# A row softmax that is bound by its transfers: tiles of twelve rows in four buffers instead of eight rows in six, with a held first store and an uninterleaved end

## The chip, the cores and the metric

The program runs on one core of one Trainium2 chip. The time is device microseconds of one execution. "Span" is the time from the first to the last instruction in a profile; the reported time is some two microseconds longer.

## The reference

```python
batch, seq, dim = 32, 512, 1024          # x: float32, temperature 0.5
scaled  = x / temperature
shifted = scaled - np.max(scaled, axis=-1, keepdims=True)
exp_x   = np.exp(shifted)
return exp_x / np.sum(exp_x, axis=-1, keepdims=True)
```

That is 16,384 rows of 1,024 float32: 67.11 MB are read and 67.11 MB are written.

## The kernel before

A tile holds eight consecutive rows in each of 128 partitions, so one partition's part of a transfer is one piece of 8 x 4 KB = 32 KB. Six such tiles are in flight. A tile is worked on in groups of four rows: VectorE takes the maximum of the group, ScalarE computes the exponentials in place and their sums, VectorE divides. Loads are issued from SyncE (the load queue), stores from ScalarE (the store queue). The load that refills a buffer waits for the store that empties it.

```python
TILES = [[8]] * 16
BUFS = 6
GROUP = 4
...
def load():                                    # next tile, if there is one
    xt = data.tile([P, sum(TILES[i]), d], f32, name="xt")
    nc.sync.dma_start(out=xt, in_=dram(xf, i))
...
def store(g):                                  # after the last group of a tile
    ...
    nc.scalar.dma_start(out=dram(of, i)[:, a : a + k, :], in_=tiles[i][:, a : a + k, :])
    if a + k == sum(TILES[i]):
        load()
...
for _ in range(BUFS):
    load()
for g in range(len(groups) + 1):
    if g < len(groups):
        maximum(g); exponential(g)             # group g ...
    if g > 0:
        divide(g - 1); store(g - 1)            # ... before the division of group g-1
```

## Time and profile before

| | kernel before |
|---|---|
| time, median of 6 runs (lowest to highest) | 317.98 us (317.84 to 318.26) |
| span of the profiled run | 316.0 us |
| loads plus stores, share of the transfer engines' time | 49.7% + 49.2% |
| VectorE, ScalarE busy | 75%, 47% |

The prediction below shows the page's first parts and the rates by window. The rows of the busy instructions, from the page's part 5 of the kernel before, are these (line, engine, operation, output and input with their shapes, count; busy us and mean ns of one; idle time before them and what ended it):

```profile
L79 ACT ACTIVATE xt<-xt,bias 128x1024 f32<-128x1024 f32 x128 | 145.4, 1137 | 136.8 <-DVE recip L91 119.4
L70 DVE TENSOR_REDUCE top<-xt 128x4 f32<-128x4096 f32 x32 | 141.3, 4416 | 62.6 <-DMA xt<-in_x_dram 62.6
L93 DVE TENSOR_SCALAR xt<-xt,recip 128x1024 f32<-128x1024 f32 x128 | 87.7, 749 | 1.1
```

A group of four rows costs VectorE 4.42 us for the maximum, 2.74 us for four divides (overlapping a little) and two small operations: one group starts 7.4 us after the last. VectorE's long waits are all for loads. So VectorE waits for the transfers; the prediction shows that the transfers hardly ever pause.

### The profile page before, as it was taken

How to read it: one execution, taken by the hardware profiler on the slowest of the kernel's cores; microseconds unless marked ns; L12 is line 12 of the kernel's file. 1: busy time of each engine (PE TensorE's matmuls, PEld its weight loads, DVE VectorE, ACT ScalarE, POOL GpSimd, SP SyncE). 2: the span in 40 equal slices, each digit the busy share in tenths (PEclk: the TensorE clock that was granted, in tenths of full speed). 3: DMA queues.
4: the chain of work that ended last, by engine and by line, in shares of the span. 5: the costliest groups of instructions: out<-in, count | busy, mean ns of one | idle time of the engine just before them, and what ended most of it. 6: DMA issues, size and time to landing. Idle time of an engine off the chain costs nothing.

```text
span 316.0 us, 620 instructions
## 1 busy us (share of the span) xinstructions
DVE 235.5 (75%) x224; ACT 149.6 (47%) x257; POOL 0.2 (0%) x4
## 2 busy tenths in 40 slices
DVE  0399999999689494994949859497693976949720
ACT  0176666666526255361554605546064560645500
POOL 0000000000000000000000000000000000000000
DMA  8999999999999999999999999999999999999996
GB/s 332 411 452 423 373 460 415 452 425 431 436 427 440 427 444 423 444 419 448 415 452 411 452 408 456 423 444 427 436 431 432 440 423 444 419 444 419 452 411 274
DMA packets 4612, 134.25 MB, mean 425 GB/s; under 512 B 512, under 2 KB 512, under 8 KB 512
## 3 DMA queue, kind: packets, MB, share of 16 engines
q1 hardware_dynamic: 2304, 67.11, 49.7%
q10 hardware_dynamic: 2304, 67.11, 49.2%
q14 instruction: 4, 0.03, 0.0%
HBM read 67.11 MB, written 67.11 MB: 425 GB/s over the span
## 4 chain that ended last, share of the span: by engine, by line
DVE 49%; DMA 32%; another core or an unknown queue 9%; ACT 5%; issue 1%; DVEq 0%; SPq 0%
DVE top L70 29%; DMA xt<-in_x_dram 20%; DVE xt L93 18%; DMA out_dram<-xt 12%; ACT xt L79 5%; DVE recip L91 1%; DVE bias L73 1%; DVEq L147 0%; SPq L61 0%
## 5 line engine op out<-in xcount | busy, mean ns | idle before, releaser
L79 ACT ACTIVATE xt<-xt,bias 128x1024 f32<-128x1024 f32 x128 | 145.4, 1137 | 136.8 <-DVE recip L91 119.4
L70 DVE TENSOR_REDUCE top<-xt 128x4 f32<-128x4096 f32 x32 | 141.3, 4416 | 62.6 <-DMA xt<-in_x_dram 62.6
L93 DVE TENSOR_SCALAR xt<-xt,recip 128x1024 f32<-128x1024 f32 x128 | 87.7, 749 | 1.1
L79 ACT ACTIVATION_READ_ACCUMULATOR xt<-xt,bias 128x1 f32 x128 | 23.9, 187 | 0.0
L79 ACT ACT_TABLE_LOAD x1 | 1.3, 1283 | 13.0 <-DMA xt<-in_x_dram 13.0
L91 DVE RECIPROCAL recip<-sums 128x4 f32<-128x4 f32 x32 | 5.5, 171 | 2.1 <-ACT xt L79 2.1
L73 DVE TENSOR_SCALAR bias<-top 128x4 f32<-128x4 f32 x32 | 5.4, 170 | 1.1
L133 POOL MEMSET const-bfloat16-1.0<- 128x1 bf16 x1 | 0.1, 101 | 0.0
L133 POOL MEMSET const-uint8-127<- 128x1 uint8 x1 | 0.1, 101 | 0.0
L133 POOL MEMSET const-float32-0.0<- 128x1 f32 x1 | 0.1, 98 | 0.2 <-issue 0.2
L133 POOL MEMSET const-float32-1.0<- 128x1 f32 x1 | 0.1, 98 | 0.0
## 6 DMA issues: line engine op xcount, KB each, us to landing
xt<-in_x_dram SPq DMA_DIRECT2D x16, 4096.0 KB, 50.2
out_dram<-xt ACTq DMA_DIRECT2D x16, 4096.0 KB, 38.6
```

Of the source, the lines that this page charges most:

```text
L70: nc.vector.tensor_reduce(out=top, in_=tiles[i][:, a : a + k, :], axis=mybir.AxisListType.X, op=extreme)
L73: nc.vector.tensor_scalar_mul(bias, in0=top, scalar1=-scale)
L79: nc.scalar.activation(tiles[i][:, a + b, :], tiles[i][:, a + b, :], mybir.ActivationFunctionType.Exp, bias=bias[:, b : b + 1], scale=scal ...
L91: nc.vector.reciprocal(recip, sums)
L93: nc.vector.tensor_scalar_mul(tiles[i][:, a + b, :], in0=tiles[i][:, a + b, :], scalar1=recip[:, b : b + 1])
L133: nc = _bacc.Bacc("TRN2", target_bir_lowering=False, num_devices=1)
```

## The change

The intent, as far as the diff tells it: fewer, longer transfers with the same 48 rows (192 KB per partition) in the buffers; a first store that doesn't start before the third load is in; and an end in which the store of the tenth tile needn't wait for the eleventh's maximum.

```diff
-TILES = [[8]] * 16
-BUFS = 6
+TILES = [[12]] * 10 + [[8]]
+BUFS = 4
@@ store
             a, k = part
+            if i == 0:
+                nc.scalar.copy(stats.tile([P, 1], f32, name="seen"), tiles[2][:, 0, 0:1])
             nc.scalar.dma_start(out=dram(of, i)[:, a : a + k, :], in_=tiles[i][:, a : a + k, :])
@@ main loop
+            alone = 0 < g < len(groups) and groups[g][0] > groups[g - 1][0] == len(TILES) - 2
+            if alone:
+                divide(g - 1)
+                store(g - 1)
             if g < len(groups):
                 maximum(g)
                 exponential(g)
-            if g > 0:
+            if g > 0 and not alone:
                 divide(g - 1)
                 store(g - 1)
```

The added copy reads one column of the third tile. It stands in ScalarE's order ahead of the store, so ScalarE reaches the store only when that tile has landed.

## The prediction

> **What bounds the kernel now.** I read the page of the profile first, for the share of each engine; then the rates in chosen windows of time, for where the transfers lose; then the waits of the load-issuing queue and the timelines of the start and the end.
>
> The page, parts 1 to 3 (engine, busy us, share; then tenths and GB/s in 40 slices; then the transfer queues):
>
> ```profile
> span 316.0 us, 620 instructions
> DVE 235.5 (75%) x224; ACT 149.6 (47%) x257; POOL 0.2 (0%) x4
> DMA  8999999999999999999999999999999999999996
> GB/s 332 411 452 423 373 460 415 452 425 431 436 427 440 427 444 423 444 419 448 415 452 411 452 408 456 423 444 427 436 431 432 440 423 444 419 444 419 452 411 274
> q1 hardware_dynamic: 2304, 67.11, 49.7%
> q10 hardware_dynamic: 2304, 67.11, 49.2%
> ```
>
> Two queues, loads (q1) and stores (q10), together take 98.9% of the sixteen transfer engines' time. No compute engine passes 75%. The kernel is bound by moving 67.11 MB in and 67.11 MB out, not by VectorE, although the chain that ended last names it for 49%: that chain runs through whatever came last at each step, while the transfers beside it never pause.
>
> The windows view (stretch, its length, busy time of each engine, clock, transfer share, GB/s) says where bytes were not moved:
>
> ```profile
> 0.00:2.50 2.50, 0.00 (x0) 0.00 (x0) 0.20 (x4) 1.00 0.76 210
> 2.50:12.00 9.50, 0.00 (x0) 0.00 (x0) 0.00 (x0) 1.00 0.90 386
> 31.60:39.50 7.90, 7.83 (x9) 5.15 (x11) 0.00 (x0) 1.00 0.97 373
> 120.00:280.00 160.00, 120.17 (x116) 78.42 (x136) 0.00 (x0) 1.00 1.00 433
> 302.00:313.00 11.00, 0.34 (x1) 0.00 (x0) 0.00 (x0) 1.00 0.99 429
> 313.00:316.00 3.00, 0.00 (x0) 0.00 (x0) 0.00 (x0) 1.00 0.05 22
> ```
>
> Over 160 us of the middle the rate is 433 GB/s with the share at 1.00: this is the full rate. Against it each stretch loses its length times (1 - rate/433): the start 1.3 + 1.0 = 2.3 us, the stretch in which the first store joins the loads 1.1 us, the end after 313 us 2.85 us, the rest sums to about -0.4 us (rounding of where packets are counted). Check: 134.22 MB / 433 GB/s = 310.0 us, and 316.0 - 310.0 = 6.0 us against 5.9 us summed. So **six microseconds in all are not full-rate transfer**, and only part of them can be had.
>
> The last store and the issue of loads:
>
> ```profile
> 302.38 0.34 ACTq L101 DMA_DIRECT2D out_dram<-xt  x1
> SPq L61 <- DMA out_dram<-xt: 224.5, 10, 53.8
> ```
>
> Each of the ten later loads waits for a store to free its buffer, 224.5 us in total. That costs nothing today: a 4 MB load takes 50.2 us (median) from issue to landing, though it moves in 9.7 us at full rate, so it stands in a long line. The last store goes out at 302.38 us, while the store before it is still moving (429 GB/s in 302 to 313 us), so the end is just covered too.
>
> **What the Trainium skill says.** "DMA: Bandwidth & Descriptors", section "Where 436 GB/s comes from", gives 435.2 GB/s as the ceiling of the ports; this case's 433 agrees, so the middle has no more to give. "HBM Reference", section "Specifications (TRN2)", says that a core alone measures about 425 GB/s, bounded by its 16 DMA engines; the page's mean is 425. "DMA: Bandwidth & Descriptors", section "Queues, rings and completion order", says each DMA engine alternates between its queues packet by packet; the trace agrees: the first load lands after 12.2 us alone, a store in the mixed middle after 38.6 us (median). The same page, "Why small descriptors are slow (HBM only)", gives a fixed cost of about three cycles per packet. No run here shows that cost yet. A packet here is one partition's rows, 67.11 MB in 2048 large packets, so 32 KB; it becomes 48 KB.
>
> **The change, part by part.**
>
> *Bytes.* None is saved: 310.0 us stay. Full-size packets per transfer engine fall from 256 to 176 (ten tiles and the short one, eight packets each, in and out). If the gap from 435.2 to 433 GB/s, about 1.5 us over the run, were all per-packet cost, the change would save 80/256 of it, 0.5 us; I count 0.3 us.
>
> *Engines.* The order of instructions is the same but for the last groups, so VectorE does the same 32 groups: maximum 4.42, bias 0.17, reciprocal 0.1, four divides 2.74, 7.4 us a group. The added copy is a one-column ScalarE operation, some 0.19 us like the 187 ns accumulator read of the same width, off the path.
>
> *Start.* A tile of twelve rows is 6.29 MB, 14.5 us at full rate. Loads end near 17, 31.5, 46 and (alone) 60.5 us. Tile 0 needs its three groups divided, and the third divide stands behind the first maximum of tile 1: from landing at 17.8 us that ends near 45 us. The third load lands at about 47 us, so the wait holds the store some 2 us. The fourth load is in line all that time, so nothing idles; the loss where the store joins (1.1 us) stays.
>
> *First refill, the new risk.* With four buffers and one load left, load 3 and store 0 share the engines from about 51 us and both are through near 75.5 us. Only now can load 4 be issued, some 1.6 us later (store 0 ended about 56 us in the kernel before and the load on its buffer issued at 57.56). Until it starts, near 82 us, the load queue is empty. Store 1 was ready at about 67.5 us (three more groups of 7.4 us after 45), so the engines move stores meanwhile and do not idle. But the load queue joins anew, and if joining costs what the first store's did, up to another 1 us; I count half, 0.4 us.
>
> *Middle.* A load and a store together take 29 us. VectorE needs 22.2 us of it. Tile i's store waits for tile i+1's landing and 7.5 us; by stepping on, store 3 is ready at about 120 us and its turn comes at 127, and so on every 29 us: a slack of some 7 us. Load 5 stands in line about 12 us before load 4 ends. The middle stays at 433 GB/s.
>
> *End.* Stepping on, load 9 ends near 257 us, store 7 near 272, store 8 near 288. Without interleaving, store 9 is issued after three maxima and the rest, 27 us after landing: about 285, in time. Then the eight-row tile: two maxima, the exponentials of 4.6 us behind them, divides: 17 us, so the last store is issued at about 301.5 us, and store 9 ends at 303. Both are in time, the second by a microsecond. After it 9.7 us and the completion, as before.
>
> *Sum.* Span 316.0 - 0.3 (packets) + 0.4 (second joining) + 0.2 (half a chance of a short hole before the last store) = 316.3. Reported times lie 2.0 us over the span (317.96 against 316.0), so about 318.3; but this was evidently arranged with care, and the lost stretches at the start of mixing and at the end may each shrink by a few tenths with fewer, longer transfers. I take 0.8 us off for that as a judgement, not a calculation: **317.5 us**.
>
> **The rivals.**
> 1. *Buffers bind.* Four buffers hold the same 192 KB per partition, but come free in lumps of 6.29 MB. If a store's turn comes before it is ready, or load 4 joins late, the engines idle once per tile: the slack of 7 us eaten and 1 us lost in each of seven tiles is 325 us, slower by over 2%. For it: the fall from 50 us of waiting line to about 12. Against it: the step-by-step slack stays positive everywhere, and VectorE has 7 us to spare per tile.
> 2. *The long packets are faster.* If the first-store loss (1.1 us) goes with the wait for the third load, packets save their 0.5 us, and nothing rejoins, the span is 314.4 and the time 316.4. For it: the wait looks made for this. Against it: the joining happens whenever two queues meet.
> 3. *The end opens.* If store 9 or the last store misses its turn by 2 us, transfers idle and the time is near 320. For it: the margin is about 1 us. Against it: the kernel before has no more margin and shows no hole.
>
> **Range and chances.** Even with every loss but first byte and completion gone, the time can fall by about 2 us, against 6.4 us for a gain over 2%; that leaves 1% for faster. A loss over 2% needs rival 1: 2%. The range 316.3 to 319.2 has rival 2 at its lower edge and part of rival 3 at its upper one.
>
> **What would show it.** Right: the middle at 433 GB/s, the page's transfer row at 9 throughout; store 0 issued at about 47 us; one gap in the loads between some 75 and 82 us filled with stores; large packets down to 1408 a queue; the last store at 301 to 303 us; VectorE's busy time unchanged near 235 us. Wrong: transfer digits under 9 once per tile (rival 1); a hole near 288 or 303 us (rival 3); a middle rate above 435 GB/s or no dip where the first store joins (rival 2); or a different rate for 48 KB packets, which nothing in the profile of before can show.

## The result

| | before | after |
|---|---|---|
| time, median (lowest to highest), 6 runs each | 317.98 us (317.84 to 318.26) | 318.54 us (318.42 to 318.89) |
| profiled run: time, span | 317.86, 316.0 us | 318.42, 316.3 us |

The ratio is 1.0018, with a 95% interval of 1.0005 to 1.0031. (Ratios here are the mean time of one kernel's fast runs over that of the other's of the same rounds, so not quite the ratio of the medians.) The changed kernel is slower by half a microsecond; by the 2% rule it is the same. (Its repeat below gave 1.0010, 0.9997 to 1.0023: the half microsecond is at the edge of the noise.) The prediction said 317.5 us, 316.3 to 319.2.

The page of the changed kernel, parts 1 to 3:

```profile
span 316.3 us, 601 instructions
DVE 235.2 (74%) x224; ACT 149.7 (47%) x258; POOL 0.2 (0%) x4
DMA  8999999999999999999999999999999999999995
GB/s 317 460 416 448 435 410 385 410 468 410 441 454 410 448 435 416 448 429 410 466 416 435 454 410 455 429 416 454 423 416 460 424 431 429 450 414 454 429 421 240
q1 hardware_dynamic: 1584, 67.11, 49.7%
q10 hardware_dynamic: 1584, 67.11, 49.0%
```

The transfers never pause after the first slice and before the last. Packets per queue are 1,584 instead of 2,304. The dip where the store queue joins has moved from the fifth slice (373) to the seventh (385). Its rates by window:

```profile
0.00:2.50 2.50, 0.00 (x0) 0.00 (x0) 0.20 (x4) 1.00 0.92 275
...
44.00:60.00 16.00, 15.86 (x17) 10.63 (x20) 0.00 (x0) 1.00 1.04 418
120.00:280.00 160.00, 122.89 (x119) 78.45 (x135) 0.00 (x0) 1.00 1.00 434
280.00:302.00 22.00, 17.75 (x19) 9.55 (x18) 0.00 (x0) 1.00 1.01 436
302.00:313.00 11.00, 0.00 (x0) 0.00 (x0) 0.00 (x0) 1.00 0.91 395
313.00:316.30 3.30, 0.00 (x0) 0.00 (x0) 0.00 (x0) 1.00 0.07 30
```

The columns are those of the prediction's windows. The stretch around the first store, 44 to 60 us, moves at 418 GB/s; the middle at 434, a hair over the 433 of before; the end is full until 313 us but for its last packets. (A window's rate counts a packet where it starts, which makes short windows scatter.)

The held first store and the last two stores, from the timeline of the changed kernel (start, length, engine, line):

```profile
47.38 0.19 ACT L104 COPY seen<-xt 128x1 f32<-128x1 f32 x1 [0.16 <-DMA xt<-in_x_dram]
47.39 0.37 ACTq L105 DMA_DIRECT2D out_dram<-xt  x1
...
283.40 0.34 ACTq L105 DMA_DIRECT2D out_dram<-xt  x1
...
300.17 0.34 ACTq L105 DMA_DIRECT2D out_dram<-xt  x1
```

The trace also records each transfer packet: its queue, start, length and size. From these records I summed, for each of the sixteen transfer engines, how far it lies behind an engine that moves 32 KB in 1.21 us without a pause. (The records don't name the engine; I chained each packet's end to the next one's start.) The means over the engines, in us:

```
                                               before   after
start: first packet and filling behind it        2.61    2.71
store queue joins the load queue                +0.82   +1.15
everything later (per-packet gain included)     +0.27   -0.07
mean of the engines at the end                   3.70    3.79
the last engine ends at                        314.80  314.99
span                                           315.99  316.32
reported time of this run                      317.86  318.42
```

The profiled pair differs by 0.56 us, as the medians do. Of it, rounded, 0.09 us are the mean engine (0.10 + 0.33 - 0.34), 0.10 the last engine's distance from the mean, 0.15 lie between the last packet and the last instruction, and 0.23 outside the span: the time is 1.87 us over the span before, 2.10 after. No instruction or packet of the span explains that last term.

### The profile page after: what moved, and what is told of

It reads as the page before. It is cut to its first block, busy times and chain, and to the rows that moved or that the text cites. A ratio compares the mean times of both kernels' runs of the same rounds, so it can differ in the third digit from the quotient of the medians.

```text
span 316.3 us, 601 instructions
## 1 busy us (share of the span) xinstructions
DVE 235.2 (74%) x224; ACT 149.7 (47%) x258; POOL 0.2 (0%) x4
## 3 DMA queue, kind: packets, MB, share of 16 engines
q1 hardware_dynamic: 1584, 67.11, 49.7%
q10 hardware_dynamic: 1584, 67.11, 49.0%
## 4 chain that ended last, share of the span: by engine, by line
DMA 56%; DVE 29%; ACT 9%; issue 1%; DVEq 0%; SPq 0%; ACTq 0%
DMA xt<-in_x_dram 29%; DMA out_dram<-xt 27%; DVE top L70 18%; DVE xt L93 10%; ACT xt L79 9%; DVE bias L73 1%; DVE recip L91 1%; DVEq L156 0%; SPq L61 0%; ACTq L79 0%
```

## The experiments

Twelve kernels were run on one chip, all correct. "Before" on that chip was 317.97 us over 11 to 13 runs (317.83 to 318.78).

### The parts, one at a time

Tiles and buffers alone (the copy taken out, `alone` always false):

```diff
-            if i == 0:
-                nc.scalar.copy(stats.tile([P, 1], f32, name="seen"), tiles[2][:, 0, 0:1])
...
-            alone = 0 < g < len(groups) and groups[g][0] > groups[g - 1][0] == len(TILES) - 2
+            alone = False
```

> Twelve-row tiles in four buffers alone; no wait of the first store, last tiles interleaved. Theory A (the 0.5 us come with the longer packets: the stretch in which the first store joins the loads loses 1.1 us instead of 0.8, the start 0.1 more, while the packets give back 0.3): the time is that of the whole change, 318.3 to 318.7, and the transfers never pause. Rival B (the wait or the order at the end costs the 0.5 us): 317.8 to 318.1. Rival C (the two other parts are what keeps twelve-row tiles from a hole at the end): over 319, with a hole in the transfers before the last store.

Tiles and the wait (only `alone = False`):

> Twelve-row tiles and the wait, last tiles interleaved. Theory A: the same as tiles alone within 0.2 us, since the fourth load is in line during the wait; the first store is issued at 47.4 us and not at about 45.4. Rival B1 (the wait costs): some 0.5 us over tiles alone. Rival B2 (the wait helps, because the first store meets only one load in line): 0.3 us or more under tiles alone, and a smaller loss between 44 and 60 us.

Tiles and the uninterleaved end (only the copy taken out):

> Twelve-row tiles, the last two tiles not interleaved, no wait. Theory A: the same as tiles alone within 0.2 us. In the whole change the store of the tenth tile was issued at 283.4 us and its turn came at 288.7; interleaved it would go out near 286 us, still in time, so the order at the end moves nothing. Rival C: interleaved, that store or the last one misses its turn, and this kernel is 1 us or more under tiles alone.

The whole change once more:

> The whole change once more, on the same chip as its parts. Theory A: within 0.2 us of tiles alone, 318.4 to 318.7, some 0.15 to 0.2% over the kernel before. If all four agree, the small loss belongs to the tiles.

| kernel | median (lowest to highest) | ratio to before (95%) |
|---|---|---|
| tiles alone | 320.32 (318.23 to 322.90) | 1.0071 (1.0034 to 1.0108) |
| tiles + wait | 318.52 (318.20 to 318.59) | 1.0010 (0.9998 to 1.0022) |
| tiles + end | 320.35 (319.57 to 321.82) | 1.0076 (1.0055 to 1.0097) |
| all | 318.45 (318.25 to 318.56) | 1.0010 (0.9997 to 1.0023) |

My theory A, that wait and end move nothing and the half microsecond belongs to the tiles, fell. Rival C, which foresaw a hole without the two other parts, came nearest; but of the two the wait alone does it. **With twelve-row tiles the wait is worth 1.8 to 1.9 us and the steadiness**; the order at the end is worth nothing measurable, with the wait or without.

What goes wrong without the wait is visible in the profile of tiles alone. First the end of its timeline (VectorE's maximum of the last tile, then the store of the tile before it), then its rates by window:

```profile
285.27 4.42 DVE L70 TENSOR_REDUCE top<-xt 128x4 f32<-128x4096 f32 x1 [2.30 <-DMA xt<-in_x_dram]
292.78 0.34 ACTq L101 DMA_DIRECT2D out_dram<-xt  x1
```

```profile
288.00:294.00 6.00, 5.93 (x8) 4.02 (x7) 0.00 (x0) 1.00 0.42 180
294.00:302.00 8.00, 6.07 (x7) 5.24 (x10) 0.00 (x0) 1.00 0.91 393
```

The tenth tile's store goes out at 292.78 us; most engines had nothing left from about 289 us, and the transfers run at 42% of capacity for six microseconds. The store is late because VectorE first waits for the last load, which is complete only at about 285 us. The engines finish that load 7.5 us apart in this run, from 277.4 to 284.9 us by the packet records; in the whole change they finish it 2.1 us apart. So the engines have fallen out of step, and a landing is as late as its slowest engine. Tiles + end shows that the order at the end does its job in such a run: its store of the tenth tile goes out at 285.18 us and no hole opens. Yet its engines end 3.6 us apart, the last at 316.2 instead of 315.0 us, and the times are no better. (That profile is of the fastest of its six runs; what the slower ones lost is not seen.) With the wait the interleaved order issues that store at 287.65 us and its turn comes at 288.7, so nothing is lost either way.

### Which packets make the joining expensive

Three kernels cut one transfer of the whole change into three of four rows, so that its packets are 16 KB:

```diff
+LOADS = {}                       # or {3: [4, 4, 4]}, or {0: [4, 4, 4]}
+STORES = {0: [4, 4, 4]}          # or {}
...
-            nc.sync.dma_start(out=xt, in_=dram(xf, i))
+            c = 0
+            for m in LOADS.get(i, [sum(TILES[i])]):
+                nc.sync.dma_start(out=xt[:, c : c + m, :], in_=dram(xf, i)[:, c : c + m, :])
+                c += m
```

(and the same loop for the store). The first store cut:

> The whole change, but the first store in three transfers of four rows, so that packets of 16 KB join the loads of 48 KB. Theory A in the form that the joining store's packets set the loss: the loss between 44 and 60 us falls from 1.1 to about 0.4 us, the time by some 0.5 us. In the form that the packets of the load being joined set it: 1.1 us stays. Rival (the loss has nothing to do with packet length, it is a fixed cost of the first store): 1.1 us stays here and in the next run.

Measured: 318.58 us, 318.05 to 322.07. In the packet records the joining costs 0.61 us instead of 1.15, as expected of the store's packets, if less (0.4 was expected). But later stretches lose 1.25 us that the whole change doesn't lose, and one run of four is 3.5 us over the median. A cheaper joining bought nothing.

The fourth load cut:

> The whole change, but the fourth load, the one that the first store joins, in three transfers of four rows. If the packets of the load set the loss where the store joins, it falls from 1.1 to about 0.4 us; if those of the store set it, it stays; the first store should also start sooner after its issue (5.0 us in the whole change, 4.5 in the kernel before), since fewer bytes are ahead of it in each engine.

Measured: 324.59 us, 321.04 to 328.69; the slowest kernel of all. (The run at 328.69 counts as slow, being over 1.5% above the fastest; the other three give a ratio of 1.0167, 1.0125 to 1.0209, called unclear.) The joining costs 1.14 us, unchanged. With the run before this speaks for the store's packets and against the load's; but tiles alone join at 0.7 us with packets just as long, so their length isn't all. What made this kernel slow is something else: each engine now alternates a load packet of 0.61 us with a store packet of 1.81 us, so the load gets a quarter of the bytes while a store is in line, and the cut fourth load lands at 92.7 us instead of 74.2. That the loop goes out of balance from there is argued, not tested. The packet records show directly that turns are taken by packets, whatever their length.

The first load cut:

> The whole change, but the first load in three transfers of four rows. Theory A: the loss of the start (first packet and the fill behind it) falls from 2.75 us of an engine, mean, to 2.5 or less, below the 2.6 of the kernel before; the time falls by 0.1 to 0.3 us, about what can be told apart. Rival: the start is a fixed latency, and nothing moves.

Measured: 317.98 us, 317.85 to 318.08, 0.5 us under the whole change. The start, though, loses 2.85 us, not less than 2.75; the reason given for the gain is wrong. This kernel's time is 1.78 us over its span, where the whole change's is 2.1: most of the difference is that unexplained term.

The kernel before with a wait of its own:

```diff
             a, k = part
+            if i == 0:
+                nc.scalar.copy(stats.tile([P, 1], f32, name="seen"), tiles[4][:, 0, 0:1])
```

> The kernel before with a wait of its first store for the fifth load, so that it meets one load in line as in the changed kernel, with packets of 32 KB still. Theory A: the loss where the store joins stays at 0.8 us, moved to some 54 us, and the time at that of the kernel before within 0.2 us. Rival (fewer loads in line make the joining cheap): the loss falls to 0.4 us or less, the time by 0.3 us or more.

Measured: 317.75 us, 317.71 to 317.80, ratio 0.9989 (0.9976 to 1.0002). The joining costs 0.7 us. One load in line instead of three makes it hardly cheaper; that is nearer to theory A's 0.8 us than to the rival's 0.4. The median is 0.2 us lower.

### When the first store is issued

If the wait works through the moment at which the first store goes out, any other delay should do, and a bad moment should spoil the kernel before too. These kernels hold the first store by ScalarE copies of rows of tile 0 onto themselves, which the store must wait for:

```diff
             a, k = part
+            if i == 0:
+                for b, m in enumerate([1024, 1024, 1024, 1024]):
+                    nc.scalar.copy(tiles[0][:, b, :m], tiles[0][:, b, :m])
```

in the changed kernel in place of its wait; three such copies, and five with one of 512 columns, in the kernel before.

> The changed kernel without the wait, but the first store held back by four ScalarE copies of tile 0's rows onto themselves, so that it is issued near 51 us, in the middle of the fourth load, and not at 45.6 us, where the third load passes into the fourth. Theory E (a first store issued while the engines pass from one load to the next puts them out of step; anywhere else it doesn't): the sixteen engines finish the fourth load within 1.5 us of each other, as with the wait (1.1 to 1.5), not 2.6 to 3.0 as without it, and the time is 318.3 to 318.7 with little spread. Rival F (only the landing of the third load as such, or luck of the chip, helps): 320 with a spread of 2 us or more, as without the wait.

> The kernel before, its first store held back by three such copies to some 37.7 us, in the middle of its fourth load: the control for the next run. Both theories: 317.7 to 318.1, engines within 1.5 us of each other at the fifth load.

> The kernel before, its first store held back by five and a half such copies to some 40.6 us, just before the fourth load passes into the fifth (41.1 us). Theory E: the engines fall out of step as in the twelve-row kernel without the wait, 2.5 us or more apart at the fifth load against 1.5, and the time rises by 0.5 us or more, with a spread. If it stays at 317.7 to 318.1 with engines in step, the passing from load to load is not what puts them out of step, or only where they are already over 1 us apart, as with packets of 48 KB (0.4 us apart in the kernel before).

The issue of the first store in the kernel before, in the same with five and a half copies, in twelve rows without a wait and in twelve rows with four copies:

```profile
32.66 0.37 ACTq L101 DMA_DIRECT2D out_dram<-xt  x1
39.61 0.38 ACTq L104 DMA_DIRECT2D out_dram<-xt  x1
45.60 0.38 ACTq L101 DMA_DIRECT2D out_dram<-xt  x1
51.24 0.37 ACTq L104 DMA_DIRECT2D out_dram<-xt  x1
```

| kernel | first store issued, us | time, median (lowest to highest) |
|---|---|---|
| twelve rows, no wait | 45.6 | 320.32 (318.23 to 322.90) |
| twelve rows, wait for the third load | 47.4 | 318.45 (318.25 to 318.56) |
| twelve rows, four copies | 51.2 | 317.98 (317.93 to 318.07) |
| before | 32.7 | 317.97 (317.83 to 318.78) |
| before, three copies | 37.5 | 318.38 (317.97 to 320.30) |
| before, five and a half copies | 39.6 | 322.78 (321.30 to 323.72) |
| before, wait for the fifth load | 51.8 | 317.75 (317.71 to 317.80) |

(The second row is the repeat of the whole change.) **Moving one instruction by seven microseconds in the kernel before, with nothing else added but six short copies on ScalarE, costs 4.8 us**, a ratio of 1.0143 (1.0116 to 1.0170). Rival F, that only the landing as such helps or that chips differ, falls: four copies do as well as the wait. (Of the 0.5 us by which they are faster, some 0.3 lie outside the span.) One control is missing: the same copies placed after the store, which would show what the copies alone cost; in the kernel with four of them they cost nothing that shows. The two windows below are the middle of the kernel with five and a half copies and of the one with three:

```profile
120.00:280.00 160.00, 118.19 (x113) 74.19 (x128) 0.00 (x0) 1.00 1.00 423
```

```profile
120.00:280.00 160.00, 119.90 (x113) 74.19 (x128) 0.00 (x0) 1.00 1.00 433
```

In the first the engines are counted as fully busy and yet move 423 GB/s: 160 x (1 - 423/433) = 3.7 us are lost in this stretch alone. The packet records show how. Transfers follow each other every 19.4 us in the kernel before and every 19.5 to 20.1 us here, in both queues, so the distance between the two queues' ends, once set, repeats for the whole run. A transfer ends on each engine with a packet of 4 bytes, which takes a turn like any other. So at the end of each transfer the other queue moves two long packets with only these 4 bytes between them (in the kernel before and in this one alike, on all sixteen engines). Here, in or just after most such double turns of the loads (154 of 170 between 60 and 265 us), a load packet takes up to 1.98 us instead of 1.21. In the kernel before the double turns cost nothing (none of 158).

My form of theory E was too sharp. I asked for engines 2.5 us or more apart at the fifth load; they were 1.7 us apart, and the time rose all the same. In the kernel with four copies I asked for 1.5 us at most at the fourth load; they were 1.8 us apart, and the time was still 317.98 us without spread. And the control was not clean: at 37.5 us two runs of six were near 320. What the three bad moments (45.6, 37.5, 39.6 us) have in common is that the store was issued 0.2 to 4.3 us before the first engine was through with the load then moving. The good ones were issued after the last engine was through with a load, by 0.4 to 0.7 us, and by 4.0 us in the kernel with four copies. That is a pattern in these runs and no rule: the kernel with the first store cut was issued at a good moment and still had one slow run of four. Why a moment is bad inside an engine is open.

### A version to beat both

The two edits that had come out lowest, together: the kernel before with its wait for the fifth load and its first load in two transfers of four rows.

> A version to beat both: eight-row tiles, six buffers, the first store waiting for the fifth load (317.75 in its run), and the first load in two transfers of four rows (which took the changed kernel from 318.45 to 317.98). If the two gains add: 317.3 to 317.6. If the second was an accident of how the engines met: 317.7 to 317.8.

Measured: 318.07 us, 317.79 to 318.77, ratio 1.0002 (0.9989 to 1.0016). The gains don't add, and the cut of the first load helps nothing here. The lowest of all the kernels is the one before with the wait alone, at 317.75 us; its interval reaches just past 1, so it is not clear of noise.

## Why the prediction was right or wrong

**Right: the bound.** Both kernels move the same bytes at the full rate from the first load to the last store, and no engine matters. This is why the range held, with some luck: the mechanism of the wait was not understood, and without the wait the same tiles take 320.3 us, outside the range. The sign was wrong too: half a microsecond of gain was forecast, half a microsecond of loss was measured.

**Right: the middle and the end.** The step-by-step schedule named load 4's gap, the stores' slack and the last stores. The first store went out at 47.39 us (predicted about 47), load 4's first packet came at 81.4 (82), the tenth tile's store at 283.4 (285), the last at 300.2 (301.5), 3 us ahead of its turn instead of one. The queues stood some 4 us differently than reckoned: load 5 was in line 5 to 7 us before load 4 was through, not 12, and store 3 was issued 12 to 14 us ahead of its turn, not 7. Neither ran dry. Rivals 1 and 3 did not come to pass in the whole change; rival 3 did in tiles alone, through engines out of step.

**Right in size: the packets.** 0.3 us were counted. (The landing times that the prediction gave for the turns by packet, 12.2 and 38.6 us, don't show them, since a store's time includes its place in the line; the packet records do.) In the records a load that is alone takes an engine 9.681 us with eight rows and 14.501 us with twelve, four-row loads take 4.862. These lie on a line: 4.82 us for each four rows and 0.042 us for each transfer (eight packets and the completion). 32 transfers have become 22, which saves 0.42 us. Without the fixed part the rate is 2.097 MB / 4.82 us = 435.1 GB/s, the ceiling that the prediction quoted.

**Mis-sized: the joining.** The prediction kept the loss where the first store joins as it was and put 0.4 us on a second joining of the load queue. The first grew from 0.82 to 1.15 us; the second cost nothing measurable (by the same sum, the lag was 3.92 us at 80 us and 3.89 at 100). That the summed span of 316.3 us came out as measured is luck: the 0.6 us for a second joining and a hole did not come; some 0.1 us at the start, 0.3 at the first joining and 0.25 at the end stood in for them.

**Wrong: the deduction of 0.8 us.** The sum came to a span of 316.3 and a time of 318.3; the measured span is 316.3 and the time 318.54. The prediction then took 0.8 us off "as a judgement", because the change looked arranged with care. Nothing in the profile carried that, and it is the whole error of the middle value but for 0.2 us. The rest is shared by the step that took the time as 2.0 us over the span for both (it is 1.87 and 2.10) and by a span some 0.1 us longer in the runs at the median than in the profiled one. (The prediction's 317.96 is the median of three other runs; the run with the span of 316.0 took 317.86.)

**Wrong: what the wait is for.** "The fourth load is in line all that time, so nothing idles" is true and was read as: the wait does nothing. Rival 2 guessed that it makes the joining cheap; it doesn't (1.15 us with the wait, 0.7 without it in tiles alone). The runs show a third thing that no rival named. Without the wait twelve-row tiles take 320.3 us and scatter over 4.7 us; in the two profiled runs engines that have fallen out of step land late or end late. The care in the change was there, but it repaired a harm that the tiles had brought, and the prediction booked it as a gain on top.

**Not settled.** What happens inside a transfer engine at a bad moment of joining; and what makes the time 1.8 us over the span in some kernels and 2.1 in others, with twelve-row tiles on both sides.

## What to carry to other kernels

When the transfer engines are full from end to end, tile sizes and buffers can gain little (here at most a part of 6 us in 316) and lose more, so reckon what of the time is not full-rate transfer before tuning, and don't add a bonus to a sum that the profile carried. In this kernel, with one load queue and one store queue, the relation that the first store sets between them repeated to the end, so the moment of the first store was a knob of its own: where yours is alike, try it a few microseconds earlier and later, and look at the spread of the runs as well as at the median. When an edit carries a wait that seems to do nothing, take it out alone and time it before believing so.

## What the Trainium skill lacked or had wrong

- No page has it: in this kernel the moment at which the second queue joins told for the whole run. The same eight-row kernel took 317.97 us with its first store issued at 32.7 us and 322.78 us at 39.6 us, with the engines counted as fully busy in both.
- "DMA: Bandwidth & Descriptors", "Queues, rings and completion order": turns by packet are as stated, but the page doesn't say that queues with packets of unequal length share the bytes unequally. Packets of 16 KB (0.61 us) beside packets of 48 KB (1.81 us) got a quarter, and a load landed at 92.7 us instead of 74.2. Nor does it say that the 4-byte packet that ends a transfer takes a turn as a long one does, so that the other queue moves two long packets around it, which was so on all sixteen engines.
- "DMA: Bandwidth & Descriptors", "Why small descriptors are slow (HBM only)": the section gives a fixed overhead per packet and treats small ones; a fixed cost per packet is seen here with large ones too. Packets of 16, 32 and 48 KB follow one another after 607, 1,209 and 1,812 ns, which leaves about 5 ns for each packet beside its bytes (0.042 us for eight and a completion).
- "Runtime: NRT & Kernel Launch", "Instruction fetch mechanics", treats instruction fetches, but not what they cost the data transfers beside them. Four fetches of 8 KB fall into the span of each (65.0 us twice, 181.9 and 240.1 in the kernel before). In both kernels each is followed within 0.35 us by one packet that is 0.27 to 0.57 us too long. As far as packets can be chained into engines, the two engines that end last in the kernel before, at 314.4 and 314.8 us where the others end by 313.8, are two with such packets; a third with one ends among the first. So the fetches may set the end; that is not shown.
